# Two-layer encoder on one core: early dots and eight rows of V moved forward, softmax z's transfers moved to SP

## The chip, the core and the metric

The kernel runs on one core of one Trainium2 chip. The core has a matmul engine (TensorE, "PE" in the profile, with its weight loads as "PEld"), VectorE ("DVE"), ScalarE ("ACT"), GpSimd ("POOL") and SyncE ("SP"), which run side by side and wait for each other through semaphores, and 16 DMA engines that all queues share. SP issues most of the transfers, POOL those whose addresses come from data (gathers). The metric is the device time of one execution in microseconds. The profile's source lines (L152 and so on) are lines of the kernel before.

## The reference, cut to what matters

Two layers work on 272 tokens of width 1024 (256 of the sequence and 16 learned ones, which are dropped at the end). Each layer has a token mixer, which this change leaves alone, and then the PEER block, in which every token picks, for each of 8 heads, 16 experts of 16,384:

```python
def peer_block(xc, w_query, sub_keys, expert_u, expert_v):
    c = xc.shape[0]
    q = (xc @ w_query).reshape(c, PEER_HEADS, 2, PEER_HALF)
    scores = jnp.einsum('chpk,pnk->chpn', q, sub_keys.astype(q.dtype))
    s1, i1 = lax.top_k(scores[:, :, 0], PEER_TOPK)
    s2, i2 = lax.top_k(scores[:, :, 1], PEER_TOPK)
    ...
    expert = idx1 * PEER_N_KEYS + idx2
    g = jax.nn.softmax(s.astype(jnp.float32), axis=-1).astype(xc.dtype)
    u = expert_u[expert]
    act = jax.nn.gelu(jnp.einsum('chkd,cd->chk', u, xc))
    v = expert_v[expert]
    return jnp.einsum('chk,chkd->cd', g * act, v)
```

After it the layer computes `layer_norm(ALPHA * h + f)`.

## The kernel before

**Dense tokens.** For most tokens the kernel does not gather experts. It multiplies all tokens by the whole of U (128 tiles of 128 experts, each 512 KB), applies gelu, weighs the result by a matrix that is zero except at the picked experts, and multiplies by the whole of V (128 tiles). U falls into two stages: **U1** (tiles 0 to 63, results in `act_a`), which runs while the top-k of the same layer is still being found, and **U2** (tiles 64 to 127, results in `act_b`; its tile number i counts from 0), in which the weights are made as well: `one_hot` builds one-hot matrices (AB, Bl) on VectorE, TensorE multiplies them (`g_unit`), and `weigh` applies them. **V** follows. U covers 240 tokens, V 224 tokens in layer 0 and 192 in layer 1.

**A weight tile.** `load` brings a tile (`raw`, four buffers) over SP's queue. `load_split` makes `hi` (rounded to the matmul type) on ScalarE (L145) and `lo`, the rest, on VectorE or POOL (L152). TensorE multiplies hi by the tokens' hi and lo, and lo by their hi: 24 matmuls in U (L180), 16 in V (L749, L753). In U1 POOL makes the lo's up to tile `LO_FROM` (41) and VectorE from then on, since VectorE works on the top-k before; in U2 and V all are VectorE's.

**The few.** The remaining tokens go in groups of 16 tokens by 8 heads, one (token, head) pair on each of 128 partitions, and gather their rows: for each k of 16, POOL's indirect DMA (`few_rows`, L1039) brings one row of 1024 for each partition (512 KB in all).
- An *early* group (tokens from 256 in layer 0, from 240 in layer 1) and layer 0's *late* group (from 240) gather rows of U and take dot products with x on VectorE (`few_mult`, L1046; x comes by `few_load`), apply gelu, multiply by softmax z (`few_weigh`), then gather rows of V and add them up, weighted (`few_add`, L1078 and L1080).
- The *drawn* groups (from 224 in layer 0; 224, 208 and 192 in layer 1) are part of the dense U. Their activations are dumped to DRAM in pieces (`few_dump`, L730 and L731, POOL), and 16 small gathers a group (`few_draw`, L1056) fetch those that were picked. Their rows of V are gathered and added like the others'.

A group's result is added to the dense sum by 8 matmuls (L788).

**Who orders what.** The tile framework's scheduler orders each engine's instructions; `tc.issue_after(ins)` puts those in its block behind `ins` on that engine. An engine runs its queue in order, so a waiting instruction holds up everything behind it. The early group's dots start at tile `DOTS_FROM` (48) of U1, one in 4/3 of a tile (`divmod(3 * (j - DOTS_FROM), 4)`), with the gather two steps ahead (`AHEAD`). `DOTS` (10) of the 16 are done there; U2 does the other six, k = 10 to 15, one in four tiles, the gather at step 0 and the product at step 2, with one row buffer. Everything that is left stands in `few_plan`, which spreads the steps evenly over V's tiles:

```python
        begin = 4
        slots = len(rows) + ahead
        at = [begin + s * (NK - 4 * JG - begin) // slots for s in range(slots)]
```

A slot gathers one row and uses the one gathered two slots before. The draws of a drawn group are spread from the end of the previous group's draws (tile 6 for the first) to three tiles before its first row of V is used.

**Softmax z.** For groups whose tokens lie among the first 256, z must be turned from (token) rows to (token, head) partitions. `few_spread` writes it to DRAM (L1018), `few_fetch` reads it back (L1022), one transfer a group: two groups in layer 0, four in layer 1. Before, POOL issued the spread at tile 56 of U1 and the fetch at tile 62. The positions ("pos") go the same way on SP at tiles 21 and 25.

**Pools.** The top-k's tiles, the early rows of U1 and softmax's tiles lie in a pool that closes at the end of U1; U2's one-hots and `act_b` take pools opened after it. x of the early group was loaded twice, at `LO_FROM` into that pool and again at the start of U2.

Of the kernel before, what the change touches and what calls it, by code (L numbers as in the profile page):

```python
# [7 lines left out]
F32 = mybir.dt.float32  # L8
# [9 lines left out]
P = 128  # L18
D = 1024
# [17 lines left out]
DOTS_FROM, DOTS, AHEAD, LO_FROM = 48, 10, 2, 41  # L37
# [25 lines left out]
class Trunk:  # L63
    def __init__(self, tc, a):
        self.tc, self.nc, self.a = tc, tc.nc, a
        self.early = []
        self.squares = []
        self.last_diag = None
        self.turn = {}
        self.pins = []  # L70
        self.ahead = {}
        self.pre = None
# [472 lines left out]
    def peer(self, layer, n, xs):  # L545
# [10 lines left out]
        with tc.tile_pool(name=f"few{layer}", bufs=1) as kp:  # L556
# [5 lines left out]
            with tc.tile_pool(name=f"top{layer}", bufs=1) as sp:  # L562
# [31 lines left out]
                def u_store(j, ps):  # L594
                    if j == LO_FROM:
                        for few in early:
                            self.few_load(sp, few, "kept", 1)
# [25 lines left out]
                    if j == JA - 6 - len(picked):  # L623
                        with tc.issue_after(last.ins):
                            self.few_spread(nc.gpsimd, near, "z", picked[0][3][:, None])
# [19 lines left out]
            with tc.tile_pool(name=f"act1{layer}", bufs=1) as ap1:  # L645
# [5 lines left out]
                self.few_load(rp, early[0], "kept", 1)  # L651
# [49 lines left out]
                def u_out(i, ps):  # L701
# [40 lines left out]
                self.few_plan(vp, early, late, drawn, scale, layer)  # L742
# [294 lines left out]
    def few_rows(self, pool, few, table, i, k, bufs):  # L1037
        t = pool.tile([P, D], F32, tag="rows", name="rows", bufs=bufs)
        self.nc.gpsimd.indirect_dma_start(  # L1039
            out=t, out_offset=None, in_=table,  # L1040
            in_offset=bass.IndirectOffsetOnAxis(ap=few["ids"][:, i, k:k + 1], axis=0))
        return t
# [5 lines left out]
    def few_dot(self, pool, few, k, hi, ahead):  # L1048
        if k >= ahead:
            self.few_mult(few, k - ahead)  # L1050
        if k < hi:
            few["rows"][k] = self.few_rows(pool, few, self.a["u_rows"], 0, k, ahead + 1)
# [12 lines left out]
    def few_load(self, pool, few, tag="wide", bufs=2):  # L1065
        few["x"] = pool.tile([P, D], F32, tag=tag, name="wide", bufs=bufs)
        self.nc.sync.dma_start(few["x"], few["kept"].rearrange("h t d -> (h t) d"))
        return True
# [4 lines left out]
    def few_add(self, vp, few, k):  # L1073
        nc = self.nc
        t, w = few["rows"].pop(k), few["act"][:, k:k + 1]
        if k == 0:
            few["out"] = vp.tile([P, D], F32, tag="wide", name="few_out", bufs=2)
# [4 lines left out]
    def few_plan(self, vp, early, late, drawn, scale, layer, ahead=2):  # L1082
        tables = self.a["u_rows"], self.a["peer_v"].rearrange("l a b d -> (l a b) d")
        rows = [(few, i, k) for few in early + late + drawn for i in range(2)
                for k in range(0 if i or few in late else TOPK, TOPK)]
# [4 lines left out]
        def step(s):  # L1090
            if s == ahead and not late:
                self.warm(AF.Abs_reciprocal_sqrt)
            if s >= ahead:
# [5 lines left out]
                else:  # L1099
                    if k == 0:  # L1100
                        self.few_weigh(few, scale)
                    self.few_add(vp, few, k)
                    if k == TOPK - 1:
                        self.sums.append((at[s] + 4, few))
            if s < len(rows):
                few, i, k = rows[s]
                if i == 0 and "loaded" not in few:
                    few["loaded"] = self.few_load(vp, few)
                few["rows"][k] = self.few_rows(vp, few, tables[i], i, k, ahead + 1)
# [260 lines left out]
```

## Time and profile before

| | us |
|---|---|
| median of 3 runs | 1794.49 |
| lowest and highest | 1786.73, 1797.14 |
| the profiled execution | 1794.43 |
| its span, first to last instruction | 1792.6 |
| U1, U2 and V of layer 0, about | 174 to 350, 350 to 552, 552 to 870 |
| U1, U2 and V of layer 1, about | 1079 to 1256, 1256 to 1459, 1459 to 1770 |

The span in 40 slices of 44.8 us, each digit the busy share in tenths; PEclk is the granted clock of TensorE:

```profile
PE   8999999999999999999998999999899999999996
DVE  7786985899997888787799869947899878888876
POOL 1101993310002445431000018952211026667420
PEclk9999999999999999999999999999999999999998
DMA  5446667865557999998541356567666569999984
```

U2 is where VectorE is busiest (slices 8 to 12 of layer 0), V where the DMA engines are (slices 13 to 18 and 33 to 38). A timeline row gives start, length, engine, line, operation, output and inputs, count, and in brackets the engine's idle time before it and what ended that.

### The profile page before, as it was taken

The numbers are of one execution on the slowest core, as the hardware profiler recorded it, in microseconds if no ns is written. First come the engines' busy times: TensorE is split into PE (matmuls) and PEld (weight loads), VectorE is DVE, ScalarE is ACT, GpSimd is POOL, SyncE is SP. The second block draws the span as 40 slices with busy tenths as digits, with TensorE's granted clock in tenths as the row PEclk, the third lists the DMA queues.
The fourth block names the chain that finished last, engine by engine and source line by source line (L and its number), as shares of the span: only waits on it lengthen the run. The fifth ranks groups of instructions, "written<-read, shape, count | busy, mean of one in ns | idle before, by whom it ended". The sixth has DMA issues, their size and how long they took to land.

```text
span 1792.6 us, 35062 instructions
## 1 busy us (share of the span) xinstructions
PE 1737.4 (97%) x13452; PEld 1675.9 (93%) x13452; DVE 1479.4 (83%) x2780; ACT 902.9 (50%) x1491; POOL 595.6 (33%) x408
## 2 busy tenths in 40 slices
PE   8999999999999999999998999999899999999996
PEld 6899999999999999999887899999899999999996
DVE  7786985899997888787799869947899878888876
ACT  5554454454444545885531645444445454544452
POOL 1101993310002445431000018952211026667420
PEclk9999999999999999999999999999999999999998
DMA  5446667865557999998541356567666569999984
GB/s 200 165 140 170 187 202 235 289 218 190 171 174 266 332 327 327 322 327 283 188 141 59 106 186 180 190 236 262 223 211 196 176 219 339 343 341 347 338 314 149
DMA packets 121112, 415.41 MB, mean 232 GB/s; under 512 B 17712, under 2 KB 19056, under 8 KB 120816
## 3 DMA queue, kind: packets, MB, share of 16 engines
q1 hardware_dynamic: 94128, 324.94, 54.4%
q0 software_dynamic: 26816, 88.23, 13.2%
q8 instruction: 106, 1.74, 0.4%
q14 instruction: 62, 0.51, 0.1%
HBM read 403.98 MB, written 9.13 MB: 230 GB/s over the span
## 4 chain that ended last, share of the span: by engine, by line
PE 77%; DVE 11%; DMA 5%; ACT 3%; issue 2%; POOL 1%; DVEq 0%; POOLq 0%; SPq 0%; ACTq 0%
PE u L180 42%; PE acc L749 16%; PE acc L753 10%; DMA raw<-peer_v 4%; PE u L216 3%; DVE lo L152 2%; DVE cy L1250 2%; DVE odd L1250 2%; PE g L689 1%; PE g L690 1%; ACT hi L145 1%; POOL lo L152 1%; PE sps L578 1%; PE acc L788 1%; DVE x L363 1%
## 5 line engine op out<-in xcount | busy, mean ns | idle before, releaser
L145 ACT ACTIVATE hi<-raw 128x1024 fp32r<-128x1024 f32 x556 | 588.3, 1059 | 617.2 <-PE u L180 212.8
L152 DVE TENSOR_TENSOR lo<-raw,hi 128x1024 fp32r<-128x1024 f32 x474 | 577.1, 1222 | 161.5 <-PE u L180 88.9
L180 PE MATMUL u<-xs,hi 128*128 128x240 f32 (+2 forms) x4544 | 570.5, 277 | 0.6 <-DVE xs L379 0.6
L180 PEld LDWEIGHTS u<-xs,hi 128*128 128x128 f32 x4544 | 539.3, 190 | 1.5 <-DVE xs L379 1.0
L749 PE MATMUL acc<-w,hi 128*128 128x448 f32 (+1 forms) x1984 | 422.8, 355 | 2.4 <-DVE w L264 1.8
L749 PEld LDWEIGHTS acc<-w,hi 128*128 128x128 f32 x1984 | 347.7, 189 | 14.3 <-DVE w L264 2.2
L180 PE MATMUL u<-xs,lo 128*128 128x240 f32 (+2 forms) x2272 | 309.5, 277 | 9.9 <-DVE lo L152 6.9
L180 PEld LDWEIGHTS u<-xs,lo 128*128 128x128 f32 x2272 | 282.0, 190 | 11.8 <-DVE lo L152 7.4
L753 PEld LDWEIGHTS acc<-w,lo 128*128 128x128 f32 x2048 | 265.7, 191 | 18.3 <-DVE lo L152 13.9
L753 PE MATMUL acc<-w,lo 128*128 128x224 f32 (+1 forms) x2048 | 270.4, 273 | 9.6 <-DVE lo L152 8.4
L152 POOL TENSOR_TENSOR lo<-raw,hi 128x1024 fp32r<-128x1024 f32 x82 | 210.4, 2580 | 105.4 <-ACT hi L145 76.0
L1039 POOL DMA_INDIRECT rows<-peer_v,ids x112 | 178.5, 1594 | 189.7 <-DVE few_out L1080 115.8
L1039 POOL DMA_INDIRECT rows<-u_rows,ids x48 | 67.3, 1402 | 218.6 <-DVE rows L1046 165.6
L1080 DVE SCALAR_TENSOR_TENSOR few_out<-rows,act,few_out 128x1024 f32<-128x1024 f32 x105 | 134.6, 1281 | 3.7 <-DMA rows<-peer_v,ids 3.7
L216 PE MATMUL u<-x,raw 128*128 128x272 f32 x480 | 115.1, 399 | 5.8 <-DMA x<-h 5.8
L216 PEld LDWEIGHTS u<-x,raw 128*128 128x128 f32 x480 | 92.8, 194 | 25.9 <-DMA raw<-w_in 5.2
L730 POOL COPY own<-act_b 128x512 f32<-128x512 f32 (+2 forms) x12 | 10.3, 863 | 247.7 <-ACT act_b L705 230.9
L1056 POOL DMA_INDIRECT act<-own,turn x64 | 74.0, 1157 | 26.0 <-issue 16.5
L696 ACT ACTIVATE act_b<-g 128x488 f32<-128x488 f32 (+35 forms) x52 | 20.2, 389 | 104.1 <-DVE act_b L659 90.6
L371 POOL TENSOR_SCALAR xs<-x,par 128x272 fp32r<-128x272 f32 (+1 forms) x4 | 3.5, 882 | 185.1 <-DVE x L363 185.1
L672 DVE TENSOR_TENSOR AB<-iota,iT 128x2048 f16<-128x2048 f16 x52 | 63.5, 1225 | 0.1
L1046 DVE SCALAR_TENSOR_TENSOR rows<-rows,wide 128x1024 f32<-128x1024 f32 x48 | 58.4, 1217 | 5.2 <-DMA rows<-u_rows,ids 5.2
(283 smaller groups left out, 1794.5 us busy)
## 6 DMA issues: line engine op xcount, KB each, us to landing
raw<-peer_u SPq DMA_DIRECT2D x256, 512.0 KB
raw<-peer_v SPq DMA_DIRECT2D x248, 512.0 KB
raw<-w_query SPq DMA_DIRECT2D x28, 512.0 KB
raw<-pw SPq DMA_DIRECT2D x22, 512.0 KB
raw<-w_in SPq DMA_DIRECT2D x16, 512.0 KB
raw<-w_out SPq DMA_DIRECT2D x8, 512.0 KB
raw<-peer_v SPq DMA_DIRECT2D x16, 256.0 KB
own<-own POOLq DMA_DIRECT2D x12, 256.0 KB
```

Of the source, the lines that this page charges most:

```text
L145: self.act_hi = nc.scalar.activation(hi, raw, AF.Copy).ins
L152: i = e.tensor_tensor(lo[:, s], raw[:, s], hi[:, s].bitcast(F32), op=OP.subtract)
L180: self.mm = nc.tensor.matmul(ps[:, :n], l[:, k, :], xs(k, r)[:, :n], start=start, stop=stop)
L216: self.mm = self.nc.tensor.matmul(ps[:, :n], raw[:, k, :], x[:, k, :n], start=k == 0, stop=k == NB - 1)
L672: nc.vector.tensor_tensor(AB.rearrange("p x c (a b) -> p (x c) a b", b=2), keys, iT[:, c0 // HC].rearrange("p x c b -> p (x c) b")[:, :, N ...
L749: self.mm = nc.tensor.matmul(acc[b][:, :2 * n].rearrange("p (a t) -> p a t", a=2), hi, w[:, :, :n], start=j == 0, stop=j == NK - JG - 1, s ...
L753: self.mm = nc.tensor.matmul(main[b][:, :n], hi if p_ else lo, w[:, i, :n], start=False, stop=j == NK - 1 and not p_, skip_group_check=True)
L1039: self.nc.gpsimd.indirect_dma_start(out=t, out_offset=None, in_=table, in_offset=bass.IndirectOffsetOnAxis(ap=few["ids"][:, i, k:k + 1], a ...
L1046: self.nc.vector.scalar_tensor_tensor(t, t, 1.0, few["x"], op0=OP.mult, op1=OP.mult, accum_out=few["act"][:, k:k + 1])
L1056: self.nc.gpsimd.indirect_dma_start(out=few["act"][:, k:k + 1], out_offset=None, in_=few["table"].rearrange("p j (t o) -> (p j t) o", o=1) ...
L1080: nc.vector.scalar_tensor_tensor(few["out"], t, w, few["out"], op0=OP.mult, op1=OP.add)
L1250: nc.vector.scalar_tensor_tensor(z, h, w, z, op0=OP.mult, op1=OP.add)
```

## The change

- **U1**: `LO_FROM` goes from 41 to 34, so VectorE makes seven more lo's and POOL seven fewer; the top-k's last steps, tied to `LO_FROM`, move with it. The early dots start at tile 41 instead of 48 and 14 instead of 10 are done there.
- **U2**: two early dots (k = 14, 15) instead of six; gelu at tile 10 instead of 24; `few_weigh` at tile 12; then eight rows (`ROWS`) of the early group's V are gathered at tiles 14, 18, ... 42 and added at 16, 20, ... 44.
- **V**: the early group gathers rows 8 to 15 only. The plan has 56 rows instead of 64 in each layer.
- **Softmax z**: spread at tile 63 of U1 and fetch at tile 6 of U2, on SP behind the newest weight load.
- **Buffers**: x of the early group is loaded once, into the layer's pool ("kept"), and the early sum takes that place when the dots are done. The other groups' sums alternate between that place and one "wide" buffer. Each row gather is put behind the one before.

```diff
-DOTS_FROM, DOTS, AHEAD, LO_FROM = 48, 10, 2, 41
+DOTS_FROM, DOTS, ROWS, AHEAD, LO_FROM = 41, 14, 8, 2, 34
...
                     if j == LO_FROM:
-                        for few in early:
-                            self.few_load(sp, few, "kept", 1)
+                        with tc.issue_after(self.last_load):
+                            self.few_load(kp, early[0], "kept")
...
-                    if j == JA - 6 - len(picked):
-                        with tc.issue_after(last.ins):
-                            self.few_spread(nc.gpsimd, near, "z", picked[0][3][:, None])
+                    if j == JA - 1:
+                        with tc.issue_after(self.last_load):
+                            self.few_spread(nc.sync, near, "z", picked[0][3][:, None])
...
-                    if j == JA - 2:
-                        with tc.issue_after(last.ins):
-                            self.few_fetch(nc.gpsimd, near, "z")
...
-                self.few_load(rp, early[0], "kept", 1)
...
                     if step == 0 and DOTS <= k < TOPK:
-                        with tc.issue_after(self.lo_ins.ins):
-                            early[0]["rows"][k] = self.few_rows(rp, early[0], a["u_rows"], 0, k, 1)
+                        early[0]["rows"][k] = self.few_rows(rp, early[0], 0, k, 1)
                     if step == 2 and DOTS <= k < TOPK:
                         with tc.issue_after(self.dve_lo.ins):
                             self.few_mult(early[0], k)
-                        if k == TOPK - 1:
-                            nc.scalar.activation(early[0]["act"], early[0]["act"], AF.Gelu_apprx_tanh)
+                    done = 2 + 4 * (TOPK - DOTS)
+                    if i == 6:
+                        with tc.issue_after(self.last_load):
+                            self.few_fetch(nc.sync, near, "z")
+                    if i == done:
+                        nc.scalar.activation(early[0]["act"], early[0]["act"], AF.Gelu_apprx_tanh)
+                    if i == done + 2:
+                        with tc.issue_after(self.dve_lo.ins):
+                            self.few_weigh(early[0], scale)
+                    k, step = divmod(i - done - 4, 4)
+                    if step == 0 and 0 <= k < ROWS:
+                        early[0]["rows"][k] = self.few_rows(rp, early[0], 1, k, 1)
+                    if step == 2 and 0 <= k < ROWS:
+                        with tc.issue_after(self.dve_lo.ins):
+                            self.few_add(early[0], k, kp, "kept")
...
-    def few_rows(self, pool, few, table, i, k, bufs):
+    def few_rows(self, pool, few, i, k, bufs):
         t = pool.tile([P, D], F32, tag="rows", name="rows", bufs=bufs)
-        self.nc.gpsimd.indirect_dma_start(
-            out=t, out_offset=None, in_=table,
-            in_offset=bass.IndirectOffsetOnAxis(ap=few["ids"][:, i, k:k + 1], axis=0))
+        table = self.a["peer_v"].rearrange("l a b d -> (l a b) d") if i else self.a["u_rows"]
+        with self.tc.issue_after(self.last_rows or self.lo_ins.ins), self.tc.issue_after(self.lo_ins.ins):
+            self.last_rows = self.nc.gpsimd.indirect_dma_start(
+                out=t, out_offset=None, in_=table,
+                in_offset=bass.IndirectOffsetOnAxis(ap=few["ids"][:, i, k:k + 1], axis=0)).ins
...
-                for k in range(0 if i or few in late else TOPK, TOPK)]
+                for k in range((ROWS if few in early else 0) if i else 0 if few in late else TOPK, TOPK)]
+        for i, few in enumerate(late + drawn):
+            few["home"] = (vp, "wide") if (i + len(late)) % 2 == 0 else (kp, "kept")
+        for few in early:
+            few["home"] = kp, "kept"
```

More of the change, by code (lines that the diff above doesn't have):

```diff
@@ L67, in __init__ @@
         self.squares = []
-        self.last_diag = None
+        self.last_diag = self.last_rows = None
         self.turn = {}
@@ L741, in peer @@
                 vp = row_pool.__enter__()
-                self.few_plan(vp, early, late, drawn, scale, layer)
+                self.few_plan(kp, vp, early, late, drawn, scale)
                 acc = [self.bank(NB - 1 - b, f"acc{b}") for b in range(NB)]
@@ L1051, in few_dot @@
         if k < hi:
-            few["rows"][k] = self.few_rows(pool, few, self.a["u_rows"], 0, k, ahead + 1)
+            few["rows"][k] = self.few_rows(pool, few, 0, k, ahead + 1)
     def few_draw(self, few, k):
@@ L1063, in few_gelu, with few_load @@
             self.warm(AF.Abs_reciprocal_sqrt)
-    def few_load(self, pool, few, tag="wide", bufs=2):
-        few["x"] = pool.tile([P, D], F32, tag=tag, name="wide", bufs=bufs)
+    def few_load(self, pool, few, tag):
+        few["x"] = pool.tile([P, D], F32, tag=tag, name="wide", bufs=1)
         self.nc.sync.dma_start(few["x"], few["kept"].rearrange("h t d -> (h t) d"))
@@ L1071, in few_weigh, with few_add @@
         self.nc.vector.scalar_tensor_tensor(few["act"], few["act"], scale, few["z"][:, 0], op0=OP.mult, op1=OP.mult)
-    def few_add(self, vp, few, k):
+    def few_add(self, few, k, pool, tag):
         nc = self.nc
@@ L1076, in few_add @@
         if k == 0:
-            few["out"] = vp.tile([P, D], F32, tag="wide", name="few_out", bufs=2)
+            few["out"] = pool.tile([P, D], F32, tag=tag, name="few_out", bufs=1)
             nc.vector.tensor_scalar(few["out"], t, w, None, op0=OP.mult)
@@ L1080, in few_add, with few_plan @@
             nc.vector.scalar_tensor_tensor(few["out"], t, w, few["out"], op0=OP.mult, op1=OP.add)
-    def few_plan(self, vp, early, late, drawn, scale, layer, ahead=2):
-        tables = self.a["u_rows"], self.a["peer_v"].rearrange("l a b d -> (l a b) d")
+    def few_plan(self, kp, vp, early, late, drawn, scale, ahead=2):
         rows = [(few, i, k) for few in early + late + drawn for i in range(2)
-                for k in range(0 if i or few in late else TOPK, TOPK)]
+                for k in range((ROWS if few in early else 0) if i else 0 if few in late else TOPK, TOPK)]
[3 more added lines that the diff above has]
+            few["home"] = kp, "kept"
         begin = 4
@@ L1101, in step @@
                         self.few_weigh(few, scale)
-                    self.few_add(vp, few, k)
+                    self.few_add(few, k, *few["home"])
                     if k == TOPK - 1:
@@ L1107, in step @@
                 if i == 0 and "loaded" not in few:
-                    few["loaded"] = self.few_load(vp, few)
-                few["rows"][k] = self.few_rows(vp, few, tables[i], i, k, ahead + 1)
+                    few["loaded"] = self.few_load(vp, few, "wide")
+                few["rows"][k] = self.few_rows(vp, few, i, k, ahead + 1)
         self.steps = [(t, lambda s=s: step(s)) for s, t in enumerate(at)]
```

## The prediction

> **What bounds the kernel now.** I read the page's busy times first, then the matmul engine's own order of instructions around each stage's edge, then tables by stretch.
>
> ```profile
> span 1792.6 us, 35062 instructions
> PE 1737.4 (97%) x13452; PEld 1675.9 (93%) x13452; DVE 1479.4 (83%) x2780; ACT 902.9 (50%) x1491; POOL 595.6 (33%) x408
> PE 77%; DVE 11%; DMA 5%; ACT 3%; issue 2%; POOL 1%; DVEq 0%; POOLq 0%; SPq 0%; ACTq 0%
> ```
>
> TensorE is busy for 97% of the span and carries 77% of the chain of waits. No part of this change removes a matmul of the weights, so it can only win back TensorE's idle time, 55 us in all, most of which lies in the mixers and norms that it leaves alone. The question is thus where TensorE idles inside U1, U2 and V. The order of TensorE's instructions at the edge from U1 to U2 of layer 1 shows the largest hole (columns: start, length, idle before):
>
> ```profile
> 1248.51 1.96 PE L180 MATMUL u<-xs,hi 128*128 128x240 f32 x16
> 1251.20 1.95 PE L180 MATMUL u<-xs,hi 128*128 128x240 f32 x16
> 1254.62 1.96 PE L180 MATMUL u<-xs,hi 128*128 128x240 f32 x16
> 1261.47 2.06 PE L180 MATMUL u<-xs,lo 128*128 128x240 f32 x8 [4.90 <-DVE lo L152]
> 1263.33 3.62 PE L180 MATMUL u<-xs,hi 128*128 128x240 f32 x16
> 1268.10 1.95 PE L180 MATMUL u<-xs,hi 128*128 128x240 f32 x16
> 1260.00:1270.00 10.00, 8.53 (x49) 8.53 (x50) 5.01 (x5) 2.86 (x4) 2.67 (x3) 0.66 0.66 245
> ```
>
> A tile of U takes 2.69 us from start to start (1251.20 − 1248.51). The next three take 3.42, 8.71 and 4.77: **8.8 us too many** (0.73 + 6.02 + 2.08). The last of these follows the idle time: the granted clock is 0.66 in those ten us, and 16 matmuls take 3.62 instead of 1.95. The other engines say why:
>
> ```profile
> 1237.11 2.22 POOL L1018 DMA_DIRECT2D z<-z  x4 [4.10 <-DVE d L957]
> 1242.74 2.21 POOL L1022 DMA_DIRECT2D z<-z  x4 [3.41 <-DMA z<-z]
> 1247.42 0.98 POOL L1039 DMA_INDIRECT rows<-u_rows,ids  x1 [0.30 <-DVE lo L152]
> 1251.19 1.23 DVE L1046 SCALAR_TENSOR_TENSOR rows<-rows,wide 128x1024 f32<-128x1024 f32 x1 [3.82 <-DMA rows<-u_rows,ids]
> 1254.92 1.22 DVE L1046 SCALAR_TENSOR_TENSOR rows<-rows,wide 128x1024 f32<-128x1024 f32 x1 [1.36 <-DMA rows<-u_rows,ids]
> 1256.19 2.36 DVE L672 TENSOR_TENSOR AB<-iota,iT 128x2048 f16<-128x2048 f16 x2
> 1260.20 2.35 DVE L152 TENSOR_TENSOR lo<-raw,hi 128x1024 fp32r<-128x1024 f32 x2
> ```
>
> POOL waits 4.10 us for softmax z, issues its eight transfers and waits 3.41 for their landing in between; behind them in POOL's queue stand the last two gathers of the early dots. VectorE, in order, waits 3.82 and 1.36 us for those, then makes the first one-hots, and only then the lo's that TensorE needs. Layer 0 has the same edge without the wait for a gather:
>
> ```profile
> 348.49 2.36 DVE L672 TENSOR_TENSOR AB<-iota,iT 128x2048 f16<-128x2048 f16 x2
> 350.32 1.96 PE L180 MATMUL u<-xs,hi 128*128 128x240 f32 x16
> 354.78 1.95 PE L180 MATMUL u<-xs,hi 128*128 128x240 f32 x16
> ```
>
> Here a tile takes 4.46 instead of 2.69, **1.8 us too many**. In the V stages the table by stretch (columns: length; busy time of PE, PEld, DVE, ACT, POOL; clock, DMA share, GB/s) gives
>
> ```profile
> 560.00:692.00 132.00, 132.00 (x843) 125.62 (x842) 109.23 (x119) 64.39 (x65) 59.62 (x41) 1.00 0.92 331
> 692.00:772.00 80.00, 77.73 (x493) 73.25 (x493) 66.07 (x70) 60.46 (x112) 37.62 (x24) 1.00 0.92 323
> 1480.00:1540.00 60.00, 56.24 (x380) 54.55 (x380) 51.81 (x61) 29.40 (x30) 39.65 (x30) 1.00 0.94 335
> 1540.00:1740.00 200.00, 197.23 (x1358) 194.64 (x1357) 172.64 (x185) 101.53 (x103) 111.12 (x78) 1.00 0.94 341
> ```
>
> TensorE idles 2.3 us in V of layer 0, and 3.8 + 2.8 in V of layer 1. The DMA engines are 92 to 94% busy throughout; at 331 GB/s there were 132 us with no idle time of TensorE at all, at 341 there is some.
>
> **The change part by part.**
>
> *The hand-over.* z's spread and fetch leave POOL for SP, and the last early dot moves from tile 63 to tile 61 (it starts at tile 41 instead of 48 and runs to k = 13, one dot in 4/3 of a tile: 41 + 20). Both causes of the layer 1 hole go, and the first one-hots start two tiles (5.4 us) earlier, where the 4.0 us from the first AB to the lo's (1256.19 to 1260.20) lie beside matmuls. The second load of the wide x at the edge goes too. On SP the moved transfers stand behind the loads of tile 63 and of U2's tile 6, each a few tiles ahead of use; the like-formed transfers of pos show what SP pays:
>
> ```profile
> 1130.34 2.55 SPq L1018 DMA_DIRECT2D pos<-idx  x4
> 1137.77 3.84 SPq L1022 DMA_DIRECT2D pos<-pos  x4
> ```
>
> That is 2.6 and 3.8 us of issue against four raw buffers, about four tiles of lead: nothing. What is late next is VectorE itself, so I leave 0.8 us of the 10.6: **−9.8 us** (bounds 0 and −10.6).
>
> *U1: seven more lo's and four more dots on VectorE.* Seven tiles are 7 × 2.69 = 18.8 us earlier. VectorE was waiting then:
>
> ```profile
> 284.16 1.22 DVE L152 TENSOR_TENSOR lo<-raw,hi 128x1024 fp32r<-128x1024 f32 x1 [22.49 <-PE u L180]
> 1188.74 1.23 DVE L152 TENSOR_TENSOR lo<-raw,hi 128x1024 fp32r<-128x1024 f32 x1 [22.51 <-PE u L180]
> ```
>
> In both layers 3.7 us of that wait are left over, so the lo's cost nothing; with less of it TensorE would wait for the tail of the top-k instead. The dots' gathers are another matter. At one per 4/3 tile the stage asks for 0.524 MB × 1.75 in 2.69 us, 341 GB/s, and does so for 14 gathers instead of 10. The raw loads already feel this:
>
> ```profile
> 320.00:330.00 10.00, 9.86 (x89) 9.67 (x87) 8.67 (x18) 4.07 (x7) 4.77 (x3) 1.00 0.93 325
> ACT hi L145 <- DMA raw<-peer_u: 35.7, 21, 4.1
> ```
>
> ScalarE's 35.7 us of waiting for raw in U1 of layer 0 cost TensorE only tenths, since the buffers run ahead. I take +0.3 us a layer, **+0.6** (bounds −1, as the gathers no longer wait behind z, and +4.6, from a rival below).
>
> *U2: two dots and eight adds instead of six dots.* Their prices are on the page:
>
> ```profile
> L1080 DVE SCALAR_TENSOR_TENSOR few_out<-rows,act,few_out 128x1024 f32<-128x1024 f32 x105 | 134.6, 1281 | 3.7 <-DMA rows<-peer_v,ids 3.7
> L1046 DVE SCALAR_TENSOR_TENSOR rows<-rows,wide 128x1024 f32<-128x1024 f32 x48 | 58.4, 1217 | 5.2 <-DMA rows<-u_rows,ids 5.2
> 400.00:500.00 100.00, 100.00 (x998) 99.55 (x997) 95.36 (x144) 49.06 (x112) 4.72 (x4) 1.00 0.55 181
> 1300.00:1400.00 100.00, 100.00 (x990) 99.58 (x989) 90.57 (x137) 49.38 (x111) 12.30 (x13) 1.00 0.63 202
> ```
>
> The adds stand at tiles 16, 20, ... 44 of U2, which is about 400 to 500 us and 1300 to 1400; three dots leave the same stretch. Net 8 × 1.28 − 3 × 1.22 = 6.6 us of VectorE. It has 4.6 us free in layer 0 and 9.4 in layer 1. Layer 0 is over by 2.0, of which its lead of a lo buffer covers about half: +1.0 (bounds 0 and +4). In layer 1 the gathers share POOL with the dumps:
>
> ```profile
> 1361.02 1.29 POOL L730 COPY own<-act_b 128x512 f32<-128x512 f32 x1 [35.02 <-ACT act_b L705]
> 1384.20 0.54 POOL L731 DMA_DIRECT2D own<-own  x1 [0.30 <-POOL own L730]
> ```
>
> Five dumps hold POOL's queue for 23 us; a gather queued within comes late to its add, and the lo's stand behind the add. The gather has four tiles (12 us) between two adds, so I take +0.5 (bounds 0 and +4). Together **+1.5**.
>
> *V: eight of 64 row gathers fewer in each layer.* The plan spreads 58 slots over 108 tiles where it spread 66. A tile moves 0.524 × (1 + 66/108) = 0.845 MB now and 0.806 then, 4.6% less: 341 GB/s becomes about 326, below the 331 at which layer 0 had no idle time, and its 323 becomes 308. Of 2.3 us in layer 0 I take **−1.5**, as ScalarE's diagonals fall in the same stretch; of the 2.8 late in layer 1, −2.0. Early in layer 1 something runs against it: drawn group 224's sixteen draws must fit before its first row, which now comes earlier, so they fall on tiles 6 to 18 instead of 6 to 28, with seven gathers between them, all on POOL.
>
> ```profile
> L1039 POOL DMA_INDIRECT rows<-peer_v,ids x15 | 23.8, 1584 | 17.6 <-DVE turn L1055 10.9 <-DVE few_out L1080 4.0 <-DVE few_out L1078 1.8
> L1056 POOL DMA_INDIRECT act<-own,turn x15 | 17.4, 1161 | 4.6 <-issue 3.0 <-DVE lo L152 0.6 <-DMA rows<-peer_v,ids 0.3
> ```
>
> With 0.3 us between instructions (4.6 / 15) the 23 need 16 × 1.46 + 7 × 1.88 = 36.5 us, and 13 tiles last 13 × 2.35 = 30.5 (82 tiles in the 197 us of the last stretch, less three sums). POOL falls 6 us behind; a row's add waits for its gather, and lo's for the add. Fewer gathers give 1.5 of the 3.8 us back and I let the lag cost 1.8, most of it covered by the gather's two slots of lead: +0.3 (bounds −3.8 and +15). V of layer 1: **−1.7**.
>
> **Sum**: −9.8 + 0.6 + 1.5 − 1.5 − 1.7 = −10.9 us. The profiled execution took 1794.43 us, 1.8 around its span of 1792.6, and the median of the runs shown is 1794.49, so no correction is needed: **1783.5 us**.
>
> **The rivals.**
>
> *The hand-over stays late* (the change does not do what it says there). The one-hots' pool lies where the top-k's pool was and needs every reader of it done, now SP's spread of z among them. If its landing, or softmax, comes after the last dot, VectorE still stands at the first one-hot. For it: VectorE is 8.67 of 10 us busy at 320 us. Against it: the spread's landing took about 3.4 us, and three tiles are there. Some 7 of the 9.8 us would be lost: 1790.5.
>
> *V gains in full.* POOL's lag is covered and the lower rate ends all waits: −2.3 and −6.5 instead of −1.5 and −1.7, 1778.
>
> *The loads of U1 starve.* If a gather and the loads share some 330 GB/s evenly while both run, a gather takes 0.524 / 165 = 3.2 us of each 3.59, and the loads get 0.657 MB where 0.700 is used: 0.043 MB short, 0.22 us at the 195 GB/s that tiles use (0.524 / 2.69), 3 us a layer over 14 gathers. The buffers hide a part; with +4.6 for both layers instead of +0.6 the time is 1787.5. For it: ScalarE's 35.7 us. Against it: 10 gathers cost TensorE little. [...] No row here shows the shares.
>
> *POOL drags VectorE in V of layer 1* (slower than before). If each of the 23 instructions takes as long as this gather, 1.68 us and 0.3 to the next, they need 45.5 us in 30.5: 15 us late.
>
> ```profile
> 1478.69 1.68 POOL L1039 DMA_INDIRECT rows<-peer_v,ids  x1 [1.82 <-DVE few_out L1078]
> ```
>  It decides once POOL takes more than 30.5 / 23 = 1.33 us apiece and the lag exceeds the lead, two slots of 1.86 tiles (8.7 us) less a landing of about 7.5 (1247.42 to 1254.92). If all of it reaches TensorE, with 3 us of slow clock after the idle time as at 1263.33, the time is 1783.5 + 15 + 3 = 1801.5, above before. [...] Against the rival: VectorE waited only 3.7 us for rows of V in the whole kernel.
>
> **How the numbers follow.** Forecast 0.45, hand-over late 0.17, V in full 0.15, loads starve 0.15, POOL drags 0.08. A measurement can tell about 0.5% from no change: below 1785.5 or above 1803.5. Faster: four fifths of the forecast, all of V in full, a little of the others, 0.55. Slower: half of the last rival, 0.05 with other accidents. Same: 0.40. The range reaches from V in full to just past the late hand-over, 1777.5 to 1792, and leaves the last rival out with some edges.
>
> **What would show it.** Right: tiles of 2.69 us through tile 64 of both layers with no TensorE wait over 1 us, no z on POOL, the first one-hot some 5 us before tile 63 ends; DMA near 326 GB/s in the late V of layer 1 with under 1 us of idle time. Wrong: a VectorE wait for rows in U2 or before an add in V of layer 1's first 20 tiles, TensorE idle at tiles 45 to 60 of U1 behind raw, or a TensorE wait for lo between 430 and 500 us. The prediction falls if the edge of layer 1 still loses over 3 us, or if V of layer 1 idles more than 6.6.

## The result, and the profile after

The changed kernel takes 1806.03 us (median of 8 runs, 1801.31 to 1810.11) against 1794.02 for the kernel before on the same chip: a ratio of 1.0069, 95% interval 1.0049 to 1.0090. It is slower by 0.7%, where 0.6% faster was forecast. Line numbers move: `few_rows` is now L1049, `few_mult` L1056, `few_add` L1090, `few_draw` L1066, `few_dump` L738 and L739, the first one-hots L668, softmax's first step L962 (L954 before), `few_spread` L1026. In the experiments whose edit adds lines, those behind the edit stand one or two further on.

The page after, its span, chain of waits and the row of U's lo matmuls:

```profile
span 1803.7 us, 35067 instructions
PE 76%; DVE 12%; DMA 4%; issue 4%; POOL 2%; ACT 2%; SPq 0%; POOLq 0%; DVEq 0%; ACTq 0%
L180 PE MATMUL u<-xs,lo 128*128 128x240 f32 (+2 forms) x2272 | 311.4, 278 | 18.5 <-DVE lo L152 15.5
```

The same row on the page of before:

```profile
L180 PE MATMUL u<-xs,lo 128*128 128x240 f32 (+2 forms) x2272 | 309.5, 277 | 9.9 <-DVE lo L152 6.9
```

TensorE's idle time in front of VectorE's lo's was to fall and has doubled, from 6.9 to 15.5 us. To see where, I took the starts of TensorE's groups of lo matmuls in each trace and measured three stretches in each layer: the **edge** (tile 56 to 70 of U), **U2** (tile 70 to 110), and **V** (first to last of its 134 groups). The rest hardly moves (tiles 40 to 56 of U1: 43.0 us before, 43.1 after in layer 0, 43.0 and 43.0 in layer 1).

| us, layer 0 / 1 | edge | U2 | V | span |
|---|---|---|---|---|
| before | 43.3 / 49.4 | 126.0 / 123.1 | 336.0 / 318.1 | 1792.6 |
| after | 49.0 / 45.8 | 127.3 / 133.7 | 332.6 / 319.2 | 1803.7 |
| difference | +5.7 / −3.6 | +1.3 / +10.6 | −3.4 / +1.1 | +11.1 |

Two of the six cells, the edge of layer 0 and U2 of layer 1, lose 16.3 us.

**The edge of layer 0.** Before the change the early group's softmax waited for nothing:

```profile
335.36 0.17 DVE L954 TENSOR_TENSOR z<-fv 128x16 f32<-128x16 f32 x1
```

The timeline after (start, length, engine; idle time before and what ended it):

```profile
336.42 0.91 SPq L1026 DMA_DIRECT2D z<-z  x2
335.90 1.22 DVE L1056 SCALAR_TENSOR_TENSOR rows<-rows,wide 128x1024 f32<-128x1024 f32 x1
341.66 0.17 DVE L962 TENSOR_TENSOR z<-fv 128x16 f32<-128x16 f32 x1 [4.54 <-DMA z<-z]
341.80 1.23 DVE L152 TENSOR_TENSOR lo<-raw,hi 128x1024 fp32r<-128x1024 f32 x1
343.08 2.06 PE L180 MATMUL u<-xs,lo 128*128 128x240 f32 x8 [3.36 <-DVE lo L152]
344.94 3.62 PE L180 MATMUL u<-xs,hi 128*128 128x240 f32 x16
```

The softmax of the early group (128x16) is the third of layer 0, and softmax has two buffers: it needs the one that SP's spread of z still reads. SP issues that spread at 336.42, behind the load of tile 63. VectorE stands 4.54 us, a lo stands behind it, TensorE idles 3.36 us, and then works at a lower granted clock (0.50 from 342.12 to 348.93 us; the next 16 matmuls take 3.62 us, not 1.95). Tiles 59 and 60 take 6.2 and 5.3 us instead of 2.69. Tile 61 takes 5.1, but by another wait: VectorE makes the first one-hots at 348.15, and TensorE idles 1.96 us for the lo behind them.

**U2 of layer 1.** POOL's queue, the add that waits for it, and TensorE:

```profile
1363.01 1.55 POOL L738 COPY own<-act_b 128x512 f32<-128x512 f32 x1
1370.41 0.65 POOL L738 COPY own<-act_b 128x512 f32<-128x512 f32 x1 [4.96 <-DMA own<-own]
...
1389.43 0.54 POOL L739 DMA_DIRECT2D own<-own  x1 [0.30 <-POOL own L738]
1390.27 1.01 POOL L1049 DMA_INDIRECT rows<-peer_v,ids  x1 [0.30 <-issue]
1394.80 1.29 DVE L1090 SCALAR_TENSOR_TENSOR few_out<-rows,act,few_out 128x1024 f32<-128x1024 f32 x1 [10.15 <-DMA rows<-peer_v,ids]
1397.27 2.06 PE L180 MATMUL u<-xs,lo 128*128 128x240 f32 x8 [7.34 <-DVE lo L152]
1399.13 3.62 PE L180 MATMUL u<-xs,hi 128*128 128x240 f32 x16
```

Five dumps stand on POOL from 1363.01 to 1389.97, the last four each waiting 3.2 to 5.0 us for the one before to leave the single `own` buffer. The next row gather stands behind all five. Its add waits 10.15 us, and TensorE idles 7.34 us behind the lo's behind the add.

**The edge of layer 1** gives back 3.6 of the 8.8 us:

```profile
1252.00 2.36 DVE L668 TENSOR_TENSOR AB<-iota,iT 128x2048 f16<-128x2048 f16 x2 [1.00 <-DMA z<-z]
1255.60 2.35 DVE L152 TENSOR_TENSOR lo<-raw,hi 128x1024 fp32r<-128x1024 f32 x2
1256.88 2.06 PE L180 MATMUL u<-xs,lo 128*128 128x240 f32 x8 [2.78 <-DVE lo L152]
1258.74 2.72 PE L180 MATMUL u<-xs,hi 128*128 128x240 f32 x16
```

No gather is waited for any more, but the first one-hots still stand ahead of two lo's (1252.00 to 1255.60), and they wait 1.00 us for z's landing.

**V.** The table by stretch after (length; busy PE, PEld, DVE, ACT, POOL; clock, DMA share, GB/s):

```profile
566.00:698.00 132.00, 132.00 (x851) 126.36 (x850) 106.54 (x119) 67.08 (x69) 57.78 (x39) 1.00 0.91 322
698.00:778.00 80.00, 80.00 (x519) 76.62 (x518) 65.81 (x65) 59.53 (x112) 33.41 (x23) 1.00 0.91 315
1550.00:1750.00 200.00, 198.01 (x1359) 196.14 (x1358) 168.42 (x175) 101.91 (x104) 92.07 (x67) 1.00 0.92 327
```

The rates fell to 322, 315 and 327 GB/s. In layer 0 TensorE's 2.3 us of idle time are gone, late in layer 1 2.0 of 2.8 are left. Layer 1's +1.1 has two parts: the first 30 groups take 79.3 us instead of 75.1, the others 239.9 instead of 243.0. Early in layer 1, tile 7 waits for its lo behind the plan's first add:

```profile
1480.69 1.12 POOL L1049 DMA_INDIRECT rows<-peer_v,ids  x1 [4.15 <-PE acc L757]
1488.25 1.28 DVE L1090 SCALAR_TENSOR_TENSOR few_out<-rows,act,few_out 128x1024 f32<-128x1024 f32 x1 [3.50 <-DMA rows<-peer_v,ids]
```

### The profile page after: what moved, and what is told of

Its sections match the earlier page's. It is cut to its first block, busy times and chain, and to the rows that moved or that the text cites. A ratio compares the mean times of both kernels' runs of the same rounds, so it can differ in the third digit from the quotient of the medians.

```text
span 1803.7 us, 35067 instructions
## 1 busy us (share of the span) xinstructions
PE 1740.9 (97%) x13452; PEld 1682.1 (93%) x13452; DVE 1498.4 (83%) x2794; ACT 901.7 (50%) x1491; POOL 550.7 (31%) x382
## 4 chain that ended last, share of the span: by engine, by line
PE 76%; DVE 12%; DMA 4%; issue 4%; POOL 2%; ACT 2%; SPq 0%; POOLq 0%; DVEq 0%; ACTq 0%
PE u L180 38%; PE acc L757 19%; PE acc L761 12%; PE u L216 3%; DVE lo L152 2%; DVE cy L1263 2%; DVE odd L1263 2%; DMA rows<-peer_v,ids 1%; DMA raw<-peer_v 1%; POOL lo L152 1%; PE g L685 1%; PE g L686 1%; PE sps L578 1%; DMA own<-own 1%; PE acc L796 1%
## 5 line engine op out<-in xcount | busy, mean ns | idle before, releaser
L152 DVE TENSOR_TENSOR lo<-raw,hi 128x1024 fp32r<-128x1024 f32 x488 | 595.4, 1223 | 152.2 <-PE u L180 53.5
L180 PE MATMUL u<-xs,lo 128*128 128x240 f32 (+2 forms) x2272 | 311.4, 278 | 18.5 <-DVE lo L152 15.5
L1049 POOL DMA_INDIRECT rows<-peer_v,ids x112 | 174.9, 1562 | 380.5 <-DVE few_out L1090 226.9
L152 POOL TENSOR_TENSOR lo<-raw,hi 128x1024 fp32r<-128x1024 f32 x68 | 176.7, 2617 | 101.5 <-ACT hi L145 74.2
L1090 DVE SCALAR_TENSOR_TENSOR few_out<-rows,act,few_out 128x1024 f32<-128x1024 f32 x105 | 134.3, 1279 | 13.6 <-DMA rows<-peer_v,ids 13.6
L1049 POOL DMA_INDIRECT rows<-u_rows,ids x48 | 62.9, 1309 | 166.4 <-DVE rows L1056 110.7
L1066 POOL DMA_INDIRECT act<-own,turn x64 | 77.8, 1216 | 31.6 <-issue 16.8
L668 DVE TENSOR_TENSOR AB<-iota,iT 128x2048 f16<-128x2048 f16 x52 | 63.1, 1217 | 1.0 <-DMA z<-z 1.0
L1056 DVE SCALAR_TENSOR_TENSOR rows<-rows,wide 128x1024 f32<-128x1024 f32 x48 | 58.5, 1219 | 0.0
L738 POOL COPY own<-act_b 128x512 f32<-128x512 f32 (+2 forms) x12 | 11.8, 986 | 147.2 <-ACT act_b L701 128.5
```

What stands on the lines that cost most here:

```text
L152: i = e.tensor_tensor(lo[:, s], raw[:, s], hi[:, s].bitcast(F32), op=OP.subtract)
L180: self.mm = nc.tensor.matmul(ps[:, :n], l[:, k, :], xs(k, r)[:, :n], start=start, stop=stop)
L668: nc.vector.tensor_tensor(AB.rearrange("p x c (a b) -> p (x c) a b", b=2), keys, iT[:, c0 // HC].rearrange("p x c b -> p (x c) b")[:, :, N ...
L1049: self.last_rows = self.nc.gpsimd.indirect_dma_start(out=t, out_offset=None, in_=table, in_offset=bass.IndirectOffsetOnAxis(ap=few["ids"][ ...
L1056: self.nc.vector.scalar_tensor_tensor(t, t, 1.0, few["x"], op0=OP.mult, op1=OP.mult, accum_out=few["act"][:, k:k + 1])
L1066: self.nc.gpsimd.indirect_dma_start(out=few["act"][:, k:k + 1], out_offset=None, in_=few["table"].rearrange("p j (t o) -> (p j t) o", o=1) ...
```

## The experiments

All kernels start from the changed one and keep what it computes, unless said otherwise. Stages come from one profiled execution each, ratios from the runs. All experiments in one table, with the two unaltered kernels run again:

| kernel | ratio to before [95%] | edge 0 / 1 | U2 0 / 1 | V 0 / 1 | span |
|---|---|---|---|---|---|
| before_again | 1.0001 [0.9977, 1.0025] | 43.2 / 46.7 | 126.0 / 123.1 | 335.5 / 320.1 | 1791.7 |
| after_again | 1.0059 [1.0039, 1.0079] | 50.6 / 42.5 | 127.3 / 130.6 | 332.6 / 310.6 | 1789.2 |
| z3 | 1.0030 [1.0017, 1.0043] | 46.2 / 42.5 | 127.2 / 132.8 | 334.6 / 313.8 | 1793.5 |
| dumps1 | 0.9998 [0.9982, 1.0015] | 51.7 / 45.8 | 127.2 / 123.1 | 332.4 / 313.4 | 1789.9 |
| begin10 | 1.0022 [1.0005, 1.0038] | 51.4 / 42.5 | 127.5 / 132.8 | 332.1 / 310.6 | 1792.3 |
| rows0 | 1.0016 [1.0001, 1.0032] | 50.4 / 45.2 | 126.0 / 123.1 | 336.9 / 315.5 | 1793.4 |
| z3_dumps1 | 0.9980 [0.9965, 0.9995] | 47.1 / 47.5 | 127.3 / 123.1 | 333.3 / 311.9 | 1785.3 |
| zearly_dumps1 | 0.9978 [0.9964, 0.9992] | 48.1 / 45.4 | 127.3 / 123.1 | 333.2 / 312.9 | 1785.6 |
| zearly_z3_dumps1_b10 | 0.9955 [0.9938, 0.9972] | 47.6 / 44.5 | 127.3 / 123.1 | 333.9 / 310.0 | 1782.1 |
| z3_dumps1_hot | 0.9949 [0.9927, 0.9971] | 42.0 / 41.0 | 130.6 / 126.1 | 332.3 / 313.4 | 1782.6 |
| z3_dumps1_hot_b10 | 0.9941 [0.9920, 0.9962] | 41.5 / 41.7 | 130.5 / 126.1 | 332.6 / 314.9 | 1782.6 |
| z3_dumps1_hot2_b10 | 0.9896 [0.9880, 0.9912] | 41.6 / 41.8 | 127.4 / 123.1 | 332.9 / 311.3 | 1775.0 |

**z3: a third buffer for softmax.**

```diff
-        z = sp.tile([P, H, K], F32, tag="z", name="z", bufs=2)
+        z = sp.tile([P, H, K], F32, tag="z", name="z", bufs=3)
```

> The changed kernel with three buffers for softmax z instead of two; nothing else. Theory: in layer 0 the third softmax takes the buffer that SP's late spread still reads, VectorE waits 4.5 us for that DMA at 337 us, TensorE idles 3.4 us and then runs at a lower clock. With a third buffer the wait of VectorE on the z transfer goes, tiles 59 and 60 of U1 in layer 0 take under 3.5 us each instead of 7.2 and 4.6, and the time falls by 5 to 7 us, to about 1800. Rival: VectorE is simply overloaded there by the four further dots, or raw is late; then the wait only takes another name, and the time stays at 1804 or more.

The timeline of z3 at the edge of layer 0, VectorE's rows and TensorE's:

```profile
336.36 1.22 DVE L1056 SCALAR_TENSOR_TENSOR rows<-rows,wide 128x1024 f32<-128x1024 f32 x1
337.50 1.22 DVE L152 TENSOR_TENSOR lo<-raw,hi 128x1024 fp32r<-128x1024 f32 x1
...
343.85 2.36 DVE L668 TENSOR_TENSOR AB<-iota,iT 128x2048 f16<-128x2048 f16 x2
347.87 2.35 DVE L152 TENSOR_TENSOR lo<-raw,hi 128x1024 fp32r<-128x1024 f32 x2
349.14 2.06 PE L180 MATMUL u<-xs,lo 128*128 128x240 f32 x8 [3.46 <-DVE lo L152]
```

The 4.54 us wait is gone and tiles 59 and 60 take 2.7 us again. But the edge still takes 46.2 us: VectorE now runs without a pause up to the one-hots, makes them from 343.85 to 347.87 ahead of two lo's that are due, and TensorE idles 3.46 us there. So the shared buffer cost the edge some 2 to 5.5 us (46.2 here and 47.1 in z3_dumps1, against 49.0 to 51.7 in the five profiles with two buffers and the late spread), and a second cause stood behind it.

**dumps1: the dumps spread between the gathers of U2.** Each dump goes behind the latest gather on POOL. U1's pieces are dumped closer together and earlier, and U2's pieces of each group four tiles behind those of the group before, instead of all at one tile.

```diff
-                        dumps.setdefault(j1 - 1 - JA if j >= JA else 16 * g + 8 * i + 3, []).append((few, j, j1))
+                        dumps.setdefault(8 * g + 4 * i + 3 if j < JA else min(j1 - 1 - JA + 4 * g, NK - JA - 1), []).append((few, j, j1))
...
-                        few_dump(*piece)
+                        with tc.issue_after(self.last_rows):
+                            few_dump(*piece)
```

> The changed kernel with the dumps of the drawn groups spread over U2, each put behind the newest row gather on POOL, so that at most two dumps stand ahead of a gather instead of five. Theory: at 1384 us of layer 1 VectorE waits 10.2 us for one gather that stood behind five dumps, and TensorE loses 10 to 11 us in two tiles to that, slow clock included. The two tiles of 11.2 and 5.7 us go and the time falls by 9 to 11 us, to about 1795.5. Rival: the eight adds are too much for VectorE in U2; then stalls of together 4 us or more remain between tiles 30 and 50 of U2 in layer 1, and the time stays above 1801.

The timeline of dumps1 in U2 of layer 1, POOL's queue and the add that had waited 10.15 us:

```profile
1367.40 0.58 POOL L740 DMA_DIRECT2D own<-own  x1 [0.30 <-POOL own L739]
1373.43 0.61 POOL L739 COPY own<-act_b 128x512 f32<-128x512 f32 x1 [5.45 <-DMA own<-own]
1374.34 0.57 POOL L740 DMA_DIRECT2D own<-own  x1 [0.30 <-POOL own L739]
1375.54 5.59 POOL L1050 DMA_INDIRECT rows<-peer_v,ids  x1 [0.64 <-DVE few_out L1091]
1387.34 1.28 DVE L1091 SCALAR_TENSOR_TENSOR few_out<-rows,act,few_out 128x1024 f32<-128x1024 f32 x1
```

The gather goes out 0.64 us after its buffer comes free, and its add waits for nothing. U2 of layer 1 takes 123.1 us, as before the change, though the eight rows are still there: all of the 10.6 us came from the order of dumps and gathers.

**rows0: no rows of V in U2** (all 16 in V's plan again). The early group's activations are then multiplied by softmax z twice, once in U2 and once in V; nothing else differs.

```diff
-DOTS_FROM, DOTS, ROWS, AHEAD, LO_FROM = 41, 14, 8, 2, 34
+DOTS_FROM, DOTS, ROWS, AHEAD, LO_FROM = 41, 14, 0, 2, 34
```

> The changed kernel with no row of V taken in U2 (ROWS = 0): U1, the moved z and the two dots in U2 as changed, V as before. Theory: the 10 to 11 us of layer 1's U2 go, early V of layer 1 idles 3 to 4 us as before the change instead of 7, while V of layer 0 loses the 2 to 3 us that it had gained; the layer 0 wait on z stays. Time 1794 to 1797. Rival: the loss in U2 comes from something else than the rows (the gelu at tile 10, z's fetch on SP, the dots): then the 11 us stay and the time is above 1802.

U2 takes 126.0 and 123.1, exactly as before, and V 336.9 and 315.5. The eight rows moved into U2 thus cost 1.3 us there in layer 0 (put down to VectorE's work, since it stays when the dumps are spread) and 7.5 to 10.6 in layer 1 (the dumps), and bring about 4 us in V of layer 0 (332.6 against 336.9). In layer 1, V takes 315.5 us here without a row fewer, in one profile, where before it took 318.1 and 320.1. Both edges stay as they were: the rows have no part in them.

**begin10: V's plan starts later in layer 1.**

```diff
-        begin = 4
+        begin = 4 if late else 10
```

> The changed kernel with the plan of V in layer 1 starting at tile 10 instead of 4, so that the sixteen draws of the first drawn group lie on 18 tiles instead of 13. Theory: the dense draws cost the early V of layer 1 some 7 us of TensorE idle time between tiles 7 and 37 (before: about 4); with 18 tiles about half of the excess comes back, and the time falls by 2 to 3 us, to about 1803.5. Rival: the row gathers' bytes set it; they are as dense or denser here, the idle time stays at 7 us and the time at 1806 or a little more.

The timeline early in V of layer 1, POOL's first gather and VectorE's first add:

```profile
1477.84 1.30 POOL L1049 DMA_INDIRECT rows<-peer_v,ids  x1 [4.04 <-PE acc L757]
1496.11 1.28 DVE L1090 SCALAR_TENSOR_TENSOR few_out<-rows,act,few_out 128x1024 f32<-128x1024 f32 x1
```

The first gathers go out about as late as ever, 10 us after V begins (1477.84 here, 1480.69 in the changed kernel, where V began at 1468.1 and 1470.8), since their buffers wait for V's first matmuls. But the first waiting add now stands 18 us behind them instead of 8, and finds its row. The first 30 groups of V take 71.8 us; in the four kernels of this table with the later start they take 71.7 to 72.0, in seven profiles with the plan at tile 4 and eight rows fewer (the changed kernel's two among them) 74.6 to 79.3, in rows0 73.7, and before the change 75.1 and 74.0. Whether the wait of the first adds or the closer draws cost the time is not separated, as the edit moves both. The gain in the ratio (1.0059 to 1.0022) is not split further: this profile also has the short edge of layer 1, which varies by itself, as the next runs show.

**after_again and before_again: both kernels unaltered**, profiled a second time.

> The changed kernel unaltered, so that its stages are measured beside its variants on one chip. Stages in us, by the starts of TensorE's groups of lo matmuls: from tile 56 to 70 of U 49.0 in layer 0 and 45.8 in layer 1 before this run, U2 of layer 1 from tile 70 to 110 133.7, the first 30 tiles of V of layer 1 79.3. Three theories are tried. Waits that the program's order sets (softmax's buffer, gather behind dumps) come back in every execution: 49 to 52 in layer 0, 133 to 134 in U2. The draws of V of layer 1 are such an order too: 79 again, and a ratio of 1.007. Rival: the 79.3 was late loads of that one execution or chip, and the first 30 tiles of V give about 75 as in the variants that don't touch them (75.3 and 74.9): a ratio near 1.004.

> The kernel before, unaltered, for its stages beside the variants'. If the stages are set by the program's order, the edge from tile 56 to 70 takes 43.3 and 49.4 again, U2 of layer 1 123.1, and V of layer 0 336 us. V of layer 1 took 318.1; the variants on this chip took 310.6 to 315.5. Theory: V of layer 1 gains about 4 us by eight gathers fewer, so it is near 318 here too. Rival: the difference lies between executions, and it is near 314 here: then the eight gathers fewer bring nothing in layer 1. Ratio 1.000.

after_again's median is 1801.15 us, but its profiled execution is the fastest of six, 1790.92, so it shows what varies: the edge of layer 1 takes 42.5 instead of 45.8, U2 130.6 instead of 133.7, V of layer 1 310.6 instead of 319.2, 15 us together, about the difference of the spans (14.5). The first one-hots wait for z 1.00 us in one execution and not at all in the other; the gather leaves the dumps 27.3 us after the first of them in one and 24.4 in the other (1363.01 to 1390.27; 1360.12 to 1384.56). Layer 0's edge and the order of the queues come back each time. V of layer 1 is 318.1 and 320.1 us before; with the change it is 310.6 to 319.2 with a mean of 313.6 in the seven profiles with the plan at tile 4 and eight rows fewer, so it does gain, by about 5 us, in most executions. How much of that the eight rows bring is open: rows0, with all rows, already took 315.5.

**z3_dumps1, zearly_dumps1 and zearly_z3_dumps1_b10: both cures together, and SP's spread two loads earlier.** The first has the edits of z3 and dumps1. The second has those of dumps1 and, instead of the third buffer, this one; the third has all of them and begin10's.

```diff
-                    if j == JA - 1:
+                    if j == JA - 3:
```

> The changed kernel with a third softmax buffer and a dump behind each gather, the first one-hots where the change has them. Putting them behind the lo's took 4.2 and 1.5 us from the edges of layers 0 and 1 (46.2 to 42.0, 42.5 to 41.0), but U2 from tile 70 to 110 took 130.6 and 126.1 with it, 127.2 and 123.1 without. Theory (VectorE's work moves with the one-hots and is paid in U2): edges 46.2 and 42.5, U2 127.2 and 123.1, span 1781 to 1783, within 2 us of the kernel with the one-hots moved (1784.37). Rival (U2's extra belongs to the dumps together with the buffer): U2 130 and 126 here too, and the span 4 to 6 us longer, 1787.

> The changed kernel with a dump behind each gather, softmax's two buffers, and SP's spread of z two loads earlier, behind the load of tile 61 instead of 63. Theory (it is the spread's landing that the third softmax of layer 0 and, in layer 1, the first one-hots wait for): the edge of layer 0 falls from 51.7 to about 46 as with a third buffer, that of layer 1 is 42.5 without a wait for z, span 1781 to 1784. Rival (SP then waits for softmax in front of raw loads, as POOL did): loads late at tiles 62 to 65, TensorE waiting for hi or lo there, edges of 50 or more.

> The same with the third softmax buffer as well and V's plan of gathers begun at tile 10 where a layer has no late group. Theory: the buffer brings nothing more once the spread is early (edges 46 and 42.5); the later plan takes tiles 7 and 13 of V of layer 1 from 3.5 to 4.5 us down to 2.4 (71.8 and 72.0 us for the first 30 tiles in both kernels that had it, 74.6 to 79.3 in the five that had not) and gives 2 to 3 us of it back between tiles 30 and 134: span 1780 to 1783. Rival: all of it is given back or more, span 1784 or above.

The edge of layer 1 missed its 42.5 us in all three. In the timeline of z3_dumps1 VectorE stands longer than ever at the first one-hots:

```profile
1250.57 2.36 DVE L668 TENSOR_TENSOR AB<-iota,iT 128x2048 f16<-128x2048 f16 x2 [2.18 <-DMA z<-z]
1255.45 2.06 PE L180 MATMUL u<-xs,lo 128*128 128x240 f32 x8 [3.97 <-DVE lo L152]
```

With the earlier spread the first one-hots of layer 1 wait for no z, and with two buffers the softmax of layer 0 still waits 1.09 us instead of 2.89 to 4.54; TensorE waits for no hi at the edges, so no harm by SP's loads shows. Yet the edges stay at 44.5 to 48.1. VectorE's timeline in zearly_dumps1:

```profile
334.25 0.17 DVE L963 TENSOR_TENSOR z<-fv 128x16 f32<-128x16 f32 x1 [1.09 <-DMA z<-z]
```

What remains ahead of the lo's is the one-hots, and the next edit tries them. On top of it come, in some executions, z's landing, in zearly_dumps1 0.84 us of waiting for a row of U, and slower matmuls after the idle time (16 in 3.62 us instead of 1.95, at 351.41 us in zearly_dumps1 behind 3.46 us of it).

**z3_dumps1_hot and z3_dumps1_hot_b10: the one-hots behind the lo's.**

```diff
-                    one_hot(c0)
+                    with tc.issue_after(self.dve_lo.ins):
+                        one_hot(c0)
```

> The changed kernel with a third softmax buffer, a dump behind each gather and the first one-hots behind the lo's that VectorE has been given by then. Theory: the three waits add up and the first one-hots are what is left of the edge: from tile 56 to 70 it takes 41.5 to 43 in layer 0 (46.2 with the buffer alone) and 40.6 to 41.5 in layer 1 (42.5), U2 of layer 1 104.1 + 19.0 = 123.1 from tile 70 to 110; span 1776 to 1780, ratio 0.992 to 0.994. Rival: VectorE has too much work before the edge whatever its order, so the one-hots only move the wait to their own products: 46 and 42.5 stay, span about 1782, ratio 0.996.

> The same with V's plan of gathers begun at tile 10 instead of 4 where a layer has no late group, so that the draws of V of layer 1 have more room before the first row. Theory (draws crowd POOL early): its first 30 tiles take 72 us instead of 75, as with this edit alone (71.8), and the rest loses under 1, as the slots lie closer: 2 to 3 us faster than without, ratio 0.990 to 0.993. Rival: 71.8 against 74.9 and 75.3 was the difference between executions, and the two kernels are within 1 us.

In layer 0 VectorE makes five lo's first, and the edges fall to 42.0 and 41.0 us, below before. But U2 takes 3.3 and 3.0 us more. The waits of TensorE there, from 370 to 480 us (in all, times, longest):

```profile
PE g L686 <- DVE AB L676: 2.0, 3, 0.8
```

The edit put every pair of one-hots behind a lo, not only the first, and the later ones lost their lead of one. The later plan by itself is within the noise of these two (1784.37 and 1781.91 us): in the profiles it takes 3.1 us from the first 30 groups of V of layer 1, and the others take 4.6 more.

**z3_dumps1_hot2_b10: only the first two one-hots moved.**

```diff
-                    one_hot(c0)
+                    with tc.issue_after(self.dve_lo.ins) if c0 < 2 * CC else nullcontext():
+                        one_hot(c0)
```

> The kernel with the third softmax buffer, a dump behind each gather, V's later plan and the first one-hots behind the lo's, but now only the first two of them; the later ones are made one ahead again, as in the change. Theory (what the moved one-hots cost in U2 is that all of them lost their lead, since U2's wide tiles 68 to 108 were up to 1 us longer with them, and the edge gains by the first two alone): edges of 41.5 to 42 in layer 0 and 41 to 41.7 in layer 1 as with all moved, U2 from tile 70 to 110 127.3 and 123.1 as with none moved, span 1775 to 1778, ratio about 0.991. Rival (VectorE's five lo's more at the edge are only lent, and U2 pays them back whatever the order of the later one-hots): U2 stays at 130.5 and 126.1, span 1782, ratio 0.994.

The same view, and the page's row of U's lo matmuls:

```profile
PE g L686 <- DVE AB L676: 0.4, 1, 0.4
```

```profile
L180 PE MATMUL u<-xs,lo 128*128 128x240 f32 (+2 forms) x2272 | 307.7, 276 | 3.5 <-POOL lo L152 3.1
```

Edges 41.6 and 41.8, U2 127.4 and 123.1: the theory holds, what the edges gain is not paid back in U2. TensorE's idle time in front of VectorE's lo's is gone from the row (15.5 us after the change, 6.9 before; the 3.1 left wait for POOL's lo's). The kernel takes 1776.40 us (1774.56 to 1778.10), a ratio of **0.9896** to before, and beats both kernels.

## Why the prediction was wrong

The forecast was 1783.5 us with a range to 1792; the time lies 14 us above its end. Step by step, against the profiled spans:

- **Hand-over, −9.8: measured +2.1** (+5.7 and −3.6). This is the step that failed first. Its premise that the 4.0 us of one-hots "lie beside matmuls" once they start two tiles earlier was wrong: VectorE came to them with at most one lo made ahead, so that much of the 4.0 us was still delay, and the 0.8 us left for "VectorE itself" as late next had to carry both layers' one-hots (with nothing else late, in z3, TensorE idles 3.46 us in layer 0 and 1.79 in layer 1). The rival of the late hand-over named a second cause: z's landing does hold the first one-hots in layer 1 in some executions (1.00 us here, 2.18 once). The edge takes 45.2 to 47.5 us in the four profiles with such a wait, 42.5 in three without it, but 44.5 and 45.4 in the two with the earlier spread, so its share is not settled. That the moved spread would also hold a softmax buffer, in layer 0, stood in neither; the landing, put at 3.4 us, came 5.2 us after the issue on SP (336.42 to 341.66). The change of queue was judged by who waits for the data, not by who waits for the buffer that the transfer reads. The size of the prize was right: with these causes removed the edges give 1.7 and 7.6 us, 9.3 of the 10.6 (6.5 against before_again, whose edge of layer 1 took 46.7).
- **U2, +1.5: measured +11.9.** Layer 0's term was right (+1.0 forecast, +1.2 to +1.5 in every kernel that kept the rows there, but for the two with all one-hots moved). Layer 1's +0.5 (bounds 0 and +4) was 7.5 to 10.6. The prediction had the place, the five dumps and their 23 us, and set against them that "the gather has four tiles (12 us) between two adds". That covers at most 12 us of delay, not 23, so the rows quoted left some 11 us open. In the run the gather's buffer came free at 1372.7, it left at 1390.27, and its add waited 10.15 us, with the lower clock after the idle time on top (0.67 from 1390 to 1400 us).
- **U1's loads, +0.6: measured nothing** (43.0 and 43.1 us for tiles 40 to 56, in all kernels). ScalarE did wait longer for raw (16.0 us from 280 to 352 us, 11.4 before), but it cost TensorE nothing there. The rival in which the loads starve falls with it; that a gather and the loads share the rate evenly was its assumption, and no run shows the shares.
- **V, −1.5 and −1.7: measured −3.4 and +1.1**, but over the profiles −2.8 in layer 0 (mean 333.0 of the eleven that gather eight rows fewer, 335.8 before) and −5.5 in layer 1 (313.6 against 319.1). The rival "V in full" (−2.3 and −6.5) was nearer in the time; the profiled execution of the changed kernel was a bad one for layer 1. That fewer gathers are the reason is borne out in layer 0 (336.9 with all rows, in rows0), but only in part in layer 1: rows0 took 315.5, so of the 5.5 us the fewer rows account for 1.9 by that profile, and the rest is open.
- **POOL dragging VectorE early in V of layer 1** was the wrong mechanism for a right place. POOL's draws took 1010 ns in the mean there, against 1194 before. What TensorE lost at tile 7 was the first add, planned 8 us behind a gather that cannot go out before V's first matmuls, and before the change it waited there as well (2.85 us for the first row and 1.37 for the second). Tiles 13, 14 and 21 lost more in some executions, with ScalarE waiting for raw; whether the denser draws or the rows beside them crowd those loads was not separated.

The terms as the last kernel has them add up: edges −9.3, U2 +1.4, V −3.1 and −6.8, together −17.8 against −17.6 in the span. By its own signs the forecast fell: the edge of layer 1 still lost 5.2 us (45.8 against 40.6 without the 8.8), and TensorE idled 7.9 us in the two stretches of V of layer 1 that lost 6.6 before (5.9 from 1490 to 1550 us, 2.0 from 1550 to 1750). It was wrong about what the change does to three queues, not about what there was to win.

## What to carry to other kernels

Before a transfer moves to another queue, ask for each buffer that it reads when that buffer is next written, and count the delay of its issue as a wait of that writer. A cover ("four tiles of lead") is worth only what it exceeds the longest stretch that stands ahead in the queue: compare the two numbers, and price the difference in full, plus what slower matmuls after the idle time may cost (16 took 3.62 us here, behind 7.34 us of it, instead of 1.95). When a block of work on an in-order engine stands ahead of what the bottleneck needs next, moving it earlier can leave the wait where it was, as it did here; put it behind the next few due items, once, and leave the later blocks their lead.

## What the runs showed of the hardware

In these traces the length of an idle time does not tell by itself whether TensorE's matmuls run slower after it. At the edge of layer 0 TensorE idled 1.72 us in after_again, and the next 16 matmuls took 3.50 us:

```profile
341.65 1.17 PE L180 MATMUL u<-xs,lo 128*128 128x240 f32 x8 [1.72 <-DVE lo L152]
342.66 3.50 PE L180 MATMUL u<-xs,hi 128*128 128x240 f32 x16
```

In the changed kernel's first profile it idled 1.96 us there, the next 16 took 1.95 us, and the granted clock was 1.00 from 349 to 359 us:

```profile
353.45 1.16 PE L180 MATMUL u<-xs,lo 128*128 128x240 f32 x8 [1.96 <-DVE lo L152]
354.45 1.95 PE L180 MATMUL u<-xs,hi 128*128 128x240 f32 x16
```

The first pays 1.5 us in its 16 matmuls, the second nothing. At the edge of layer 1 it is the same: behind 1.83 us of idle time 16 matmuls took 3.27 us in zearly_z3_dumps1_b10 (1256.32), behind 1.79 us they took 1.96 in z3 (1255.55). So a wait of about the same length can cost one execution 1.3 to 1.5 us more than another. What decides it was not shown.

A gather's issue on POOL took 5.59 us in dumps1 (row above, 1375.54), where z3_dumps1 has the same gather at 1.21. VectorE ran without a pause beside the start of the long one (1375.20 to 1380.25). But of the 160 row gathers in the changed kernel's first profile, one of 0.94 us (326.51) lay beside a VectorE that was busy throughout, as did the two longest, of 5.60 and 5.59 us (470.18 and 483.37). What made this one long stays open.
